# Input weights through a ring of eight slots, a second accumulator buffer, and other durations in the scheduler of a hybrid attention layer

## The chip, the cores and the metric

The kernel runs on one core of a Trainium2 chip. The metric is the device time of one launch in microseconds (us), the median of several runs. The engines are TensorE (PE in the profile; PEld is its weight load), VectorE (DVE), ScalarE (ACT), GpSimd (POOL) and SyncE (SP), which issues the DMAs. Each engine works through its own instructions in a fixed order; an instruction that has to wait holds up all that stand behind it on its engine.

## The reference

One decoder layer on x of 1024 rows (tokens) by 2048 columns, in float32:

```
h    = rms_norm(x, norm_w)
proj = h @ w_in                      # 2048 x 8208: q, k, v, gate of differential attention (8 heads),
                                     # q, k, v, z, b, a of gated DeltaNet (8 heads)
A: softmax(q1 k1) - lam * softmax(q2 k2), causal, with a relative bias, times v; rms_norm; * silu(gate)
B: causal convolution (width 4) and silu on q, k, v; q, k normalised; chunked delta rule with decay
   and beta (a triangular inverse per chunk, then a scan over the chunks); rms_norm; * silu(z)
out = rms_norm(x + concat(A, B) @ w_out, final_norm_w)
```

## The kernel before

**Startup.** x is loaded in eight blocks of 128 rows, normalised, transposed, and turned into seven right-hand operands (B11, T2, T3, T1, B21, T4, B22), each split into a high and a low float16 half.

**Input projection.** The product with w_in is made by a Strassen-like scheme: four quarter blocks of the weights (A11, A21, A12, A22, each 128 x 8 x 128 float32, 512 KB) and the sums S1 to S4 of them give seven products instead of eight. Such a group is a *job* (32 jobs, 224 products; two blocks of 128 columns each). A product is 24 matmuls of 512 columns (high by high, high by low, low by high, each over 8 row blocks) into one of two PSUM banks `prod`.

Task `weights` (line 700) prepares the operands. For each job it loads the four blocks into slots named `raw`, takes the sum of squares of each on ACT (`square`, in the trace ACT `jkw<-raw`), adds these up over the partitions with a 4-column matmul (`side<-ssq,ones`) and makes a power-of-two scale per column block; then ACT scales the blocks (`raw<-raw`), POOL makes S1 to S4, and `wsplit` makes the halves: `whi` on ACT, `wlo` (the remainder) on DVE or POOL. `wsplit` of product g waits until product g - 2 has been issued. The squares of the next job are taken between the splits of the present one: load A11 after the split of its product 2, load A21 and square A11 after that of 3, and so on (lines 727 to 742). There are six slots, one for each of A11, A21, S1, A12, A22, S2 of a job.

Task `collect` (line 843) drains a product from PSUM into four accumulators q, U, V, o on DVE, and hands the finished quarters to a consumer (`sink`).

**What the consumers do**, in the order of the jobs: DeltaNet keys (convolution, Gram matrices; at the end a triangular inverse of 62 dependent steps on DVE, tiles `A` and `tmp`, and a merge), values and gates and queries and keys of attention, written to DRAM; then attention; z; and queries and values of the DeltaNet, with the scan over 64 chunks (8 heads by 8). Attention goes through 128 units (head, block of 128 queries, map): scores into `bank` (four PSUM banks), the maximum on DVE (`nm`), the exponential on ACT (`prob`), the mixture on DVE, transposes on PE (`side`), a split (`ah`, `al`) and the product with v (`av`). The first query block of the DeltaNet (`head_state`, line 1416) waits until the last attention unit is done, because its tiles lie in memory that attention uses.

**Output projection.** The same scheme with w_out, in fp32r, then the last norm.

**What sets the order.** A planner (line 175) issues the instructions of 19 lanes of tasks one after the other, always the one that can start first by its own estimates: a cost per instruction (line 94), a time at which inputs are seen, and for a DMA its size by 360 GB/s and fixed times (line 296), with all DMAs one behind the other and at most eight under way. All of it runs while the program is built; what the chip gets is a fixed order for each engine.

Of the kernel before, what the change touches and what calls it, by code (L numbers as in the profile page):

```python
# [17 lines left out]
ALU = mybir.AluOpType  # L18
# [51 lines left out]
def parts_of(name, block):  # L70
    """A tile's name, or the names of its blocks where the planner follows these."""
# [7 lines left out]
class Op:  # L79
    """An instruction that is still to be issued."""  # L80
# [44 lines left out]
class Choice:  # L125
    """The same computation on either of two engines, the second preferred by so many microseconds."""
# [14 lines left out]
class Copy:  # L141
    """A DMA that is still to be issued."""
# [8 lines left out]
class Lane:  # L151
    """Tasks (generators of instructions and conditions) that are issued one after the other."""
# [21 lines left out]

class Planner:
    """Orders the instructions of several lanes by an estimate of when each can start."""

    def __init__(self, tc, lanes):
        self.tc, self.nc = tc, tc.nc
        self.free = dict(pe=0.0, act=0.0, dve=0.0, pool=0.0, queue=0.0, dma=0.0)  # L180
# [6 lines left out]
        self.now = 0.0  # L187
        self.margin = lambda: 0.8
# [3 lines left out]

# [24 lines left out]
    def seen(self, ends, eng):  # L217
        """When eng can see what others ended."""
        return max((t + HOP.get((e, eng), 0.0) for e, t in ends.items() if e != eng), default=0.0)

    def freed(self, name, eng):
        """When eng can see that the slot of a tile is free."""
        return max((t + HOP.get((e, eng), 0.0) for e, t in self.base.get(name.partition("@")[0], {}).items()), default=0.0)

    def ready(self, op):
        return max(self.free[op.eng], self.due(op))
# [23 lines left out]
    def pick(self, op):  # L250
        """The instruction and when it can start."""
# [10 lines left out]
    def do(self, op):  # L262
        op, t0 = self.pick(op)
        assert t0 < INF
        t1 = t0 + op.cost()
        self.free[op.eng] = t1
        self.recent[op.eng] = (op.out.name, *span(op.out), t1)
# [19 lines left out]
    def start(self, d):  # L287
# [8 lines left out]
        size = free_len(d.out) * d.out.shape[0] * 4  # L296
        t1 = max(t0 + q + 0.65, self.free["dma"]) + max(size / 360e3, 0.05)
        self.free["dma"] = t1
        self.ring = self.ring[1:] + [t1 + 0.9]
        self.wr[o] = {"dma": max(t1 + 0.8, self.wr.get(o, {}).get("dma", 0.0))}  # L300
        rd = self.rd.setdefault(i, {})
        rd["dma"] = max(t1 + 0.8, rd.get("dma", 0.0))
# [36 lines left out]
class Pool:  # L339
    """A tile pool whose slots the planner follows."""  # L340
# [29 lines left out]
def hybrid_trunk(ctx: ExitStack, tc: tile.TileContext, a, out):  # L370
# [275 lines left out]
    # (operands of the narrow product, the rows of its weights, the column group of the sum)  # L646
# [52 lines left out]

    def weights():  # L700
        cur = None
        for j in range(len(jobs) + 1):
            nxt = {"j": j} if j < len(jobs) else None
            cols = jobs[j][0] if nxt is not None else None

            def load(n):
                c, g = {"A11": (0, 0), "A12": (0, 1), "A21": (1, 0), "A22": (1, 1)}[n]
                t = nxt[n] = wp.tile([P, NH, P], F32, "raw", 6)
                dma(t, w_v[:, g * NH:(g + 1) * NH, cols[c]:cols[c] + P])

            def square(n, k):
                return act.activation(junk(D // 2).rearrange("p (a c) -> p a c", a=NH), nxt[n], AF.Square,
                                      accum_out=nxt["ssq"][:, k:k + 1])
# [1136 lines left out]
```

## Time and profile before

| | us |
|---|---|
| median of 3 runs | 2399.9 |
| lowest, highest | 2394.6, 2416.65 |
| span of the profiled execution | 2387.7 |
| PE, DVE, ACT, POOL busy | 1985.4, 1755.1, 1211.8, 1033.0 |

The profile is of one execution. Its span goes from the first to the last instruction; the measured times hold a few microseconds around it (the median of the runs is 12.2 above the span). Busy times of PE come from modelled ends of pipelined matmuls. The stages: startup to about 100 us, keys to 410, inverse and merge to 690, attention to 1493, scan to 1990 (all with products of the input projection between), output projection to the end.

### The profile page before, as it was taken

The numbers are of one execution on the slowest core, as the hardware profiler recorded it, in microseconds if no ns is written. First come the engines' busy times: TensorE is split into PE (matmuls) and PEld (weight loads), VectorE is DVE, ScalarE is ACT, GpSimd is POOL, SyncE is SP. The second block draws the span as 40 slices with busy tenths as digits, with TensorE's granted clock in tenths as the row PEclk, the third lists the DMA queues.
The fourth block names the chain that finished last, engine by engine and source line by source line (L and its number), as shares of the span: only waits on it lengthen the run. The fifth ranks groups of instructions, "written<-read, shape, count | busy, mean of one in ns | idle before, by whom it ended". The sixth has DMA issues, their size and how long they took to land.

```text
span 2387.7 us, 29240 instructions
## 1 busy us (share of the span) xinstructions
PE 1985.4 (83%) x10029; PEld 1201.5 (50%) x10029; DVE 1755.1 (74%) x2841; ACT 1211.8 (51%) x2506; POOL 1033.0 (43%) x696
## 2 busy tenths in 40 slices
PE   3778886788798879788888889978888998899986
PEld 2534443333355445444455445445555556677765
DVE  6868875999628657566677675666666768899998
ACT  6645553343346546555555555645555654333344
POOL 5633552433322322332233223424433436687885
PEclk7898998999899999899999999989999999999998
DMA  6253446332664554544445454234443444613303
GB/s 192 43 117 102 117 133 158 90 101 74 153 163 115 141 118 110 116 120 122 101 126 150 94 103 73 71 86 86 72 83 85 98 131 153 223 62 108 108 33 141
DMA packets 287044, 267.12 MB, mean 112 GB/s; under 512 B 51552, under 2 KB 225840, under 8 KB 285488
## 3 DMA queue, kind: packets, MB, share of 16 engines
q1 hardware_dynamic: 286896, 265.26, 43.6%
q8 instruction: 79, 1.29, 0.2%
q14 instruction: 69, 0.57, 0.1%
HBM read 189.66 MB, written 77.12 MB: 112 GB/s over the span
## 4 chain that ended last, share of the span: by engine, by line
DVE 34%; PE 25%; DMA 22%; ACT 7%; issue 5%; SPq 3%; POOL 3%; POOLq 0%; ACTq 0%; DVEq 0%
PE prod L273 17%; DMA raw<-in_w_in_dram 16%; PE bank L273 5%; DVE wlo L273 5%; SPq L303 3%; DVE tmp L273 3%; DVE acc L273 2%; DVE qT L273 2%; DVE A L273 2%; PE av L273 2%; PE side L273 2%; ACT jkw L273 2%; DVE whi L273 2%; DVE raw L273 1%; DVE c L273 1%
## 5 line engine op out<-in xcount | busy, mean ns | idle before, releaser
L273 PEld LDWEIGHTS <-whi 128*128 128x128 f16 x3680 | 366.7, 102 | 405.0 <-issue 85.8
L273 POOL TENSOR_TENSOR raw<-raw 128x1024 f32<-128x1024 f32 x127 | 324.1, 2559 | 126.3 <-ACT raw L273 71.6
L273 POOL TENSOR_TENSOR wlo<-raw,whi 128x1024 f16<-128x1024 f32 x78 | 183.3, 2350 | 396.2 <-ACT whi L273 384.2
L273 ACT ACTIVATE whi<-raw 128x1024 f16<-128x1024 f32 x224 | 235.0, 1050 | 106.9 <-PE prod L273 91.8
L273 PEld LDWEIGHTS <-wlo 128*128 128x128 f16 x1840 | 187.7, 102 | 198.1 <-issue 29.4
L273 ACT ACTIVATE jkw<-raw 128x1024 bf16<-128x1024 f32 x134 | 141.1, 1053 | 282.4 <-DMA raw<-in_w_in_dram 281.2
L273 DVE TENSOR_TENSOR wlo<-raw,whi 128x1024 f16<-128x1024 f32 x146 | 217.1, 1488 | 51.3 <-ACT whi L273 50.3
L273 PE MATMUL bank<-kst,qst 128*128 128x512 f32 (+3 forms) x384 | 123.6, 423 | 43.7 <-DMA kst<-kdl 19.1
L273 ACT ACTIVATE raw<-raw,sc 128x1024 f32<-128x1024 f32 x128 | 143.0, 1140 | 24.3 <-DVE sc L273 24.3
L273 PE MATMUL prod<-B21h,whi 128*128 128x512 f16 x256 | 107.0, 418 | 11.2 <-DVE V L273 11.2
L273 PE MATMUL prod<-T2h,whi 128*128 128x512 f16 (+1 forms) x280 | 104.0, 375 | 14.3 <-ACT whi L273 11.9
L273 DVE TENSOR_REDUCE nm<-bank 128x1 f32<-128x512 f32 (+2 forms) x192 | 106.6, 555 | 10.7 <-ACT prob L273 4.5
L273 PE MATMUL prod<-T2h,wlo 128*128 128x512 f16 (+1 forms) x280 | 104.3, 376 | 7.8 <-DVE wlo L273 7.8
L273 PE MATMUL prod<-T1h,whi 128*128 128x512 f16 x256 | 103.7, 405 | 6.0 <-DVE U L273 6.0
L273 PE MATMUL prod<-B21l,whi 128*128 128x512 f16 x256 | 107.7, 421 | 0.0
L273 PE MATMUL prod<-B21h,wlo 128*128 128x512 f16 x256 | 107.3, 419 | 0.0
L273 PEld LDWEIGHTS bank<-kst,qst 128*128 128x128 f32 x384 | 71.9, 208 | 66.4 <-ACT prob L273 21.0
L273 PE MATMUL prod<-T1h,wlo 128*128 128x512 f16 x256 | 103.9, 406 | 0.0
L273 PE MATMUL prod<-T2l,whi 128*128 128x512 f16 (+1 forms) x280 | 103.6, 374 | 0.0
L273 PE MATMUL prod<-T1l,whi 128*128 128x512 f16 x256 | 103.4, 404 | 0.0
L273 PE MATMUL prod<-B11h,whi 128*128 128x512 f16 (+1 forms) x280 | 101.4, 366 | 2.0 <-DVE V L273 2.0
L273 PE MATMUL prod<-B11h,wlo 128*128 128x512 f16 (+1 forms) x280 | 101.0, 365 | 2.2 <-POOL wlo L273 2.2
(458 smaller groups left out, 5477.1 us busy)
## 6 DMA issues: line engine op xcount, KB each, us to landing
raw<-in_w_in_dram SPq DMA_DIRECT2D x128, 512.0 KB, 8.8
qst<-qd SPq DMA_DIRECT2D x256, 64.0 KB, 3.2
xt<-in_x_dram SPq DMA_DIRECT2D x8, 1024.0 KB, 9.5
qd<-c SPq DMA_DIRECT2D x32, 256.0 KB, 3.5
B11h<-mixed SPq DMA_DIRECT2D x5, 1024.0 KB, 7.9
T2h<-in_w_out_dram SPq DMA_DIRECT2D x5, 1024.0 KB, 7.4
e<-grow SPq DMA_DIRECT2D x8, 512.0 KB, 10.4
kd<-y SPq DMA_DIRECT2D x8, 512.0 KB, 6.0
```

The source lines that it names most:

```text
L273: op.fn(*op.args, **op.kw)
L303: self.nc.sync.dma_start(out=d.out, in_=d.in_)
```

## The change

Three things, and the order that follows from them:

- The weight blocks go through eight slots in one sequence A11, A21, S1, A12, A22, S2 over all jobs. Eight places are taken at the start (six of them loads); each split of the products 2 to 6 of a job, and the making of S3, takes the next place, and a place of the A blocks asks for its load. The squares stay where they were.
- U gets two buffers for all jobs; before, two jobs had a second tile U1. The scratch for software DMA descriptors is set to 1024 bytes.
- The planner gets other durations: a DMA by the length of its contiguous runs, PE at half speed after little work, and one port that certain DVE and all larger POOL instructions share.

Lines with descriptions that only went away are left out.

```diff
+LAND = 0.8
...
+def transfer(d):
+
+    size = free_len(d.out) * d.out.shape[0] * 4
+    runs = [run_dram(v) if v.space == DRAM else run_of(v) for v in (d.out, d.in_)]
+    run = min(min(runs), 16384)
+    packets = size / run
+    each = 0.004 + run / 25.5e3
+    if d.in_.name.startswith('in_w_in') and run <= 512:
+        each = 0.09
+    elif run <= 512:
+        each *= 1.3
+    return max(packets * each / 16, 0.05)
...
+def ported(op):
+
+    sb = [v for v in op.aps if v.space != PSUM and free_len(v) > 1]
+    if op.eng == "pool":
+        return op.name not in ("memset", "affine_select")
+    if op.eng != "dve":
+        return False
+    if op.name in ("tensor_tensor", "scalar_tensor_tensor"):
+        return len(sb) > 1
+    return op.name in ("tensor_copy", "tensor_scalar") and bool(sb) and op.out.space != PSUM
...
+class Clock:
...
+    def run(self, t0, cost):
...
     def ready(self, op):
-        return max(self.free[op.eng], self.due(op))
+        t = max(self.free[op.eng], self.due(op))
+        if t < INF and ported(op):
+            t = max(t, self.free["port"])
+        return t
...
-        t1 = t0 + op.cost()
+        t1 = self.clock.run(t0, op.cost()) if op.eng == "pe" else t0 + op.cost()
         self.free[op.eng] = t1
+        if ported(op):
+            self.free["port"] = t1
...
-        size = free_len(d.out) * d.out.shape[0] * 4
-        t1 = max(t0 + q + 0.65, self.free["dma"]) + max(size / 360e3, 0.05)
+        t1 = max(t0 + q + 0.65, self.free["dma"]) + transfer(d)
         self.free["dma"] = t1
         self.ring = self.ring[1:] + [t1 + 0.9]
-        self.wr[o] = {"dma": max(t1 + 0.8, self.wr.get(o, {}).get("dma", 0.0))}
+        self.wr[o] = {"dma": max(t1 + LAND, self.wr.get(o, {}).get("dma", 0.0))}
         rd = self.rd.setdefault(i, {})
-        rd["dma"] = max(t1 + 0.8, rd.get("dma", 0.0))
+        rd["dma"] = max(t1 + LAND, rd.get("dma", 0.0))
...
+    RAWS = 8
+
     def weights():
+        made = {}
+
+        def state_of(j):
+            return made.setdefault(j, {"j": j}) if j < len(jobs) else None
+
+        def room(j, n):
+
+            st = state_of(j)
+            if st is None:
+                return
+            t = st[n] = wp.tile([P, NH, P], F32, "raw", RAWS)
+            if n[0] == "A":
+                c, g = int(n[2]) - 1, int(n[1]) - 1
+                c, g = {"A11": (0, 0), "A12": (0, 1), "A21": (1, 0), "A22": (1, 1)}[n]
+                c0 = jobs[j][0][c]
+                dma(t, w_v[:, g * NH:(g + 1) * NH, c0:c0 + P])
+
+        RING = ("A11", "A21", "S1", "A12", "A22", "S2")
+        place = [0]
+
+        def advance(n=1):
+            for _ in range(n):
+                j, k = divmod(place[0], len(RING))
+                place[0] += 1
+                room(j, RING[k])
+
+        def square(st, n, k):
+            return act.activation(junk(D // 2).rearrange("p (a c) -> p a c", a=NH), st[n], AF.Square,
+                                  accum_out=st["ssq"][:, k:k + 1])
+
+        def wsplit(st, idx):
+            g = 7 * st["j"] + idx
+            yield lambda: issued[0] >= g - 2
+            n = ORDER[idx][0]
+            hi = wp.tile([P, NH, P], F16, "whi", 3)
+            lo = wp.tile([P, NH, P], F16, "wlo", 3)
+            yield act.activation(hi, st[n], AF.Copy)
+            yield Choice(*(e.tensor_tensor(out=lo, in0=st[n], in1=hi, op=ALU.subtract) for e in (dve, pool)),
+                         lean=0.7)
+            ready_w[g] = hi, lo
+
+        yield when("loads")
+        advance(RAWS)
         cur = None
         for j in range(len(jobs) + 1):
-            nxt = {"j": j} if j < len(jobs) else None
-            cols = jobs[j][0] if nxt is not None else None
-
-            def load(n):
-                c, g = {"A11": (0, 0), "A12": (0, 1), "A21": (1, 0), "A22": (1, 1)}[n]
-                t = nxt[n] = wp.tile([P, NH, P], F32, "raw", 6)
-                dma(t, w_v[:, g * NH:(g + 1) * NH, cols[c]:cols[c] + P])
-
-            def square(n, k):
-                return act.activation(junk(D // 2).rearrange("p (a c) -> p a c", a=NH), nxt[n], AF.Square,
-                                      accum_out=nxt["ssq"][:, k:k + 1])
+            nxt = state_of(j)
 
             def scaled(n, c):
                 return act.activation(nxt[n], nxt[n], AF.Copy, scale=nxt["s"][:, c:c + 1])
-
-            def wsplit(st, idx):
-                g = 7 * st["j"] + idx
-                yield lambda: issued[0] >= g - 2
-                n = ORDER[idx][0]
-                hi = wp.tile([P, NH, P], F16, "whi", 3)
-                lo = wp.tile([P, NH, P], F16, "wlo", 3)
-                yield act.activation(hi, st[n], AF.Copy)
-                yield Choice(*(e.tensor_tensor(out=lo, in0=st[n], in1=hi, op=ALU.subtract) for e in (dve, pool)),
-                             lean=0.7)
-                ready_w[g] = hi, lo
 
             def either(**kw):
                 ops = [e.tensor_tensor(**kw) for e in (dve, pool)]
                 return Choice(*ops, lean=W_LEAN) if nxt["j"] == 0 else ops[1]
 
-            if j == 0:
-                yield when("loads")
             for i in range(7):
                 if cur is not None and i < 5:
                     yield from wsplit(cur, i + 2)
+                    advance()
                 if nxt is None:
                     continue
                 if i == 0:
                     nxt["ssq"] = wp.tile([P, 4], F32, "ssq", 2)
-                    load("A11")
+                    yield square(nxt, "A11", 0)
                 elif i == 1:
-                    load("A21")
-                    yield square("A11", 0)
+                    yield square(nxt, "A21", 2)
                 elif i == 2:
-                    nxt["S1"] = wp.tile([P, NH, P], F32, "raw", 6)
-                    load("A12")
-                    yield square("A21", 2)
+                    yield square(nxt, "A12", 1)
                 elif i == 3:
-                    load("A22")
-                    yield square("A12", 1)
-                elif i == 4:
-                    yield square("A22", 3)
+                    yield square(nxt, "A22", 3)
                 elif i == 5:
...
-                    s2 = nxt["S2"] = wp.tile([P, NH, P], F32, "raw", 6)
-                    yield either(out=s2, in0=nxt["S1"], in1=nxt["A11"], op=ALU.subtract)
+                    yield either(out=nxt["S2"], in0=nxt["S1"], in1=nxt["A11"], op=ALU.subtract)
                     nxt["S3"] = nxt["A21"]
                     yield either(out=nxt["S3"], in0=nxt["A11"], in1=nxt["A21"], op=ALU.subtract)
+                    advance()
                     yield scaled("A12", 0)
...
+    EV = {"q": 1, "U": 2, "V": 1, "o": 1}
+
     def ev_tile(name):
-        flags = users.get(name, [])
-        yield lambda: all(flags)
-        users[name] = []
-        return box["kp" if name == "U1" else "ev"].tile([P, 512 + HALO], F32, name)
+        history, bufs = users.setdefault(name, []), EV[name]
+        yield lambda: len(history) < bufs or all(history[-bufs])
+        history.append([])
+        return box["ev"].tile([P, 512 + HALO], F32, name, bufs)
 
     def consume(name, task):
-        flags = users[name]
+        flags = users[name][-1]
...
-        over = "U1" if j in (1, 3) else "U"
...
-            U = acc_["U"] = yield from ev_tile(over)
+            U = acc_["U"] = yield from ev_tile("U")
...
-                    acc_load(wp, "raw", 6, 0, tb, (0,))
+                    acc_load(wp, "raw", RAWS, 0, tb, (0,))
...
-    nc = bacc.Bacc("TRN2", target_bir_lowering=False, num_devices=1)
+    nc = bacc.Bacc("TRN2", target_bir_lowering=False, num_devices=1, dynamic_dma_scratch_size=1024)
```

All engines' rows move. Two places show what the prediction speaks of.

The first is SP, startup. `raw<-in_w_in_dram` are the weight loads, `xt` the blocks of x. Before:

```order
L303 DMA xt<-in_x_dram 128x2048 x2
L303 DMA gdn_w<-in_gdn_norm_w_dram 128x1
L303 DMA sub_w<-in_da_subln_w_dram 128x1
L303 DMA raw<-in_w_in_dram 128x8x128 x2
L303 DMA xt<-in_x_dram 128x2048
L303 DMA raw<-in_w_in_dram 128x8x128 x2
L303 DMA xt<-in_x_dram 128x2048 x3
L303 DMA raw<-in_w_in_dram 128x8x128 x2
L303 DMA cw<-in_conv_w_dram 96x128
L303 DMA alb<-in_a_log_dram 128x8
```

and now:

```order
L396 DMA xt<-in_x_dram 128x2048 x2
L396 DMA gdn_w<-in_gdn_norm_w_dram 128x1
L396 DMA sub_w<-in_da_subln_w_dram 128x1
L396 DMA raw<-in_w_in_dram 128x8x128 x6
L396 DMA xt<-in_x_dram 128x2048 x4
L396 DMA raw<-in_w_in_dram 128x8x128
L396 DMA cw<-in_conv_w_dram 96x128
L396 DMA alb<-in_a_log_dram 128x8
L396 DMA dtb<-in_dt_bias_dram 128x8
L396 DMA raw<-in_w_in_dram 128x8x128 x2
```

Six weight loads stand ahead of the fifth block of x, two before; with them the first two blocks of the second job are on their way, which before were asked for only in the course of the first.

The second is PE, in attention's sixth head, fifth query block (`bank<-kst,qst` are scores of 512 and 128 columns, `prod` products of the input projection, `side`, `av` and `oT` the later steps of attention). Before:

```order
L273 MATMUL av<-ident,oT 128x128 x2
L273 MATMUL side<-ident,prob 128x128
L273 MATMUL bank<-kst,qst 128x512 x2
L273 LDWEIGHTS wlo
L273 MATMUL prod<-T2h,wlo 128x512
L273 LDWEIGHTS whi
L273 MATMUL prod<-T3h,whi 128x512
L273 LDWEIGHTS whi
L273 MATMUL prod<-T3l,whi 128x512
L273 MATMUL side<-ident,prob 128x128 x3
L273 MATMUL bank<-kst,qst 128x128 x2
L273 LDWEIGHTS wlo
```

and now:

```order
L367 LDWEIGHTS wlo
L367 MATMUL prod<-T2h,wlo 128x512
L367 MATMUL bank<-kst,qst 128x512 x2
L367 MATMUL bank<-kst,qst 128x128 x2
L367 MATMUL av<-ident,oT 128x128 x2
L367 MATMUL bank<-kst,qst 128x512 x2
L367 MATMUL av<-ah,vv 128x256
L367 MATMUL bank<-kst,qst 128x128 x2
L367 MATMUL bank<-kst,qst 128x512 x2
L367 MATMUL av<-ah,vv 128x256
L367 MATMUL av<-al,vv 128x256
```

Before, the products run on between the steps of attention. Now the `prod` row here is the last for 240 rows: the remaining 128 of the 384 score matmuls, and all of attention that belongs to them, stand without a product between.

## Rows read from the trace of the kernel before

**Rows 1.** Stretch, length; busy PE, PEld, DVE, ACT, POOL (instructions); clock, DMA, GB/s.

```profile
0.00:100.00 100.00, 46.32 (x555) 41.60 (x556) 80.62 (x123) 62.32 (x108) 67.45 (x63) 0.78 0.45 129
100.00:410.00 310.00, 257.21 (x1223) 129.27 (x1219) 220.16 (x377) 156.00 (x309) 128.57 (x80) 0.91 0.50 123
410.00:690.00 280.00, 224.85 (x1151) 107.33 (x1151) 227.83 (x235) 112.58 (x151) 111.97 (x47) 0.91 0.41 107
690.00:1493.00 803.00, 685.26 (x3427) 391.26 (x3425) 526.39 (x1060) 450.00 (x1013) 230.81 (x193) 0.94 0.50 117
1493.00:1990.00 497.00, 430.03 (x2296) 268.59 (x2294) 331.82 (x606) 275.81 (x678) 203.55 (x141) 0.95 0.42 96
1990.00:2388.00 398.00, 341.76 (x1390) 263.48 (x1390) 368.32 (x442) 155.12 (x251) 290.64 (x176) 0.95 0.31 112
```

**Rows 2.** ACT's waits (total us, times, longest): span, 690 to 1493, 1493 to 1990.

```profile
ACT jkw L273 <- DMA raw<-in_w_in_dram: 281.2, 75, 12.1
ACT jkw L273 <- DMA raw<-in_w_in_dram: 117.9, 29, 8.4
ACT jkw L273 <- DMA raw<-in_w_in_dram: 44.6, 11, 12.1
```

**Rows 3.** Timeline, 830 to 849: start us, us, instruction [idle before, releaser].

```profile
830.87 0.39 SPq L303 DMA_DIRECT2D raw<-in_w_in_dram  x1
...
838.92 0.38 PE L273 MATMUL prod<-B21h,wlo 128*128 128x512 f16 x1
...
845.94 1.06 ACT L273 ACTIVATE jkw<-raw 128x1024 bf16<-128x1024 f32 x1 [7.27 <-DMA raw<-in_w_in_dram]
...
847.14 0.59 PE L273 MATMUL side<-ssq,ones 128*128 128x4 f32 x2 [6.76 <-ACT jkw L273]
...
848.59 0.65 PE L273 MATMUL prod<-B21h,wlo 128*128 128x512 f16 x1
```

**Rows 4.** DMA issues: count, KB each, median us from issue to landing.

```profile
raw<-in_w_in_dram SPq DMA_DIRECT2D x128, 512.0 KB, 8.8
```

**Rows 5.** Stretches, tile prod alone: busy PE, PEld, DVE, ACT (instructions); clock.

```profile
100.00:410.00 310.00, 231.06 (x963) 0.00 (x0) 29.27 (x40) 3.67 (x6) 0.91 0.50 123
410.00:690.00 280.00, 202.44 (x845) 0.00 (x0) 26.39 (x36) 3.37 (x5) 0.91 0.41 107
690.00:1493.00 803.00, 531.09 (x2123) 0.00 (x0) 64.87 (x89) 8.78 (x13) 0.94 0.50 117
1493.00:1990.00 497.00, 369.43 (x1407) 0.00 (x0) 43.68 (x59) 5.34 (x8) 0.95 0.42 96
690.00:791.00 101.00, 79.70 (x340) 0.00 (x0) 10.30 (x14) 1.34 (x2) 0.98 0.55 146
```

**Rows 6.** Instructions of tile wlo: ns min/median/max, first and last start us.

```profile
L273 DVE TENSOR_TENSOR wlo<-raw,whi x146: 1203/1225/3390, 75.0 to 1960.9; 128x1024 f16<-128x1024 f32 x146
```

**Rows 7.** Stretch 410 to 690, tile A (the inverse) alone: busy DVE.

```profile
410.00:690.00 280.00, 154.47 (x129) 0.91 0.41 107
```

**Rows 8.** Attention's tiles bank, side, av: busy PE, PEld, DVE, ACT.

```profile
690.00:1493.00 803.00, 123.58 (x384) 71.92 (x384) 210.76 (x432) 121.14 (x384) 0.94 0.50 117
690.00:1493.00 803.00, 57.07 (x312) 42.78 (x312) 52.56 (x92) 43.99 (x80) 0.94 0.50 117
690.00:1493.00 803.00, 106.50 (x608) 86.15 (x608) 14.87 (x31) 56.01 (x224) 0.94 0.50 117
```

**Rows 9.** DVE's waits in the attention stretch.

```profile
DVE al L273 <- ACT ah L273: 53.3, 33, 7.1
DVE bank L273 <- DMA bias<-bvec: 36.8, 7, 9.1
DVE ss L273 <- ACT jkw L273: 29.7, 18, 5.4
...
DVE U L273 <- DMA qd<-U: 5.5, 1, 5.5
```

**Rows 10.** SP's waits (the DMA queue's own), whole span.

```profile
SPq L303 <- DVE wlo L273: 73.3, 19, 20.8
```

More of the change, by code (lines that the diff above doesn't have):

```diff
@@ L172, in advance, with run_of, run_dram, __init__ @@
         return moved
+LAND = 0.8
+def run_of(ap):
+    n = 1
+    for s, k in reversed(list(ap.ap)[1:]):
+        if k == 1:
+            continue
+        if s != n:
+            break
+        n *= k
+    return 4 * n
+def run_dram(ap):
+    n = 1
+    for s, k in reversed(list(ap.ap)):
+        if k == 1:
+            continue
+        if s != n:
+            break
+        n *= k
+    return 4 * n
+def transfer(d):
[9 more added lines that the diff above has]
+    return max(packets * each / 16, 0.05)
+PORT_1 = ("tensor_copy", "tensor_scalar", "memset")
+def ported(op):
[7 more added lines that the diff above has]
+    return op.name in ("tensor_copy", "tensor_scalar") and bool(sb) and op.out.space != PSUM
+WINDOW = 3.4133
+class Clock:
+    def __init__(self):
+        self.window, self.work, self.half = 0, 0.0, True
+    def to(self, t):
+        while t >= (self.window + 1) * WINDOW:
+            share = self.work / WINDOW
+            self.half = share < (0.8 if self.half else 0.45)
+            self.window, self.work = self.window + 1, 0.0
+    def run(self, t0, cost):
+        self.to(t0)
+        t, left = t0, cost
+        while left > 1e-9:
+            edge = (self.window + 1) * WINDOW
+            rate = 0.5 if self.half else 1.0
+            d = min(left / rate, edge - t)
+            if d <= 1e-9:
+                self.to(edge)
+                t = max(t, edge)
+                continue
+            self.work += d
+            left -= d * rate
+            t += d
+            self.to(t)
+        return t
 class Planner:
@@ L179, in __init__ @@
         self.tc, self.nc = tc, tc.nc
-        self.free = dict(pe=0.0, act=0.0, dve=0.0, pool=0.0, queue=0.0, dma=0.0)
+        self.free = dict(pe=0.0, act=0.0, dve=0.0, pool=0.0, queue=0.0, dma=0.0, port=0.0)
         self.wr, self.rd, self.base, self.after = {}, {}, {}, {}
@@ L187, in __init__ @@
         self.now = 0.0
+        self.clock = Clock()
         self.margin = lambda: 0.8
@@ L225, in ready @@
     def ready(self, op):
-        return max(self.free[op.eng], self.due(op))
+        t = max(self.free[op.eng], self.due(op))
+        if t < INF and ported(op):
+            t = max(t, self.free["port"])
+        return t
     def due(self, op):
@@ L777, in weights @@
                     yield either(out=nxt["S1"], in0=nxt["A21"], in1=nxt["A22"], op=ALU.add)
-                    s2 = nxt["S2"] = wp.tile([P, NH, P], F32, "raw", 6)
-                    yield either(out=s2, in0=nxt["S1"], in1=nxt["A11"], op=ALU.subtract)
+                    yield either(out=nxt["S2"], in0=nxt["S1"], in1=nxt["A11"], op=ALU.subtract)
                     nxt["S3"] = nxt["A21"]
                     yield either(out=nxt["S3"], in0=nxt["A11"], in1=nxt["A21"], op=ALU.subtract)
+                    advance()
                     yield scaled("A12", 0)
-                else:
+                elif i == 6:
                     yield from wsplit(nxt, 1)
@@ L906, in collect @@
             drained[0] += 1
-            consume(over, sink(0, 1, U))
+            consume("U", sink(0, 1, U))
     Gc = small("Gc", [P, H, NT])
```

## The prediction

> **What bounds the kernel now.** I read four views, from coarse to fine. First the stretches of the span [rows 1]: from 100 to 1990 us TensorE (PE) is busy for 82 to 87% of each stretch, no other engine is, except VectorE (DVE) at 81% from 410 to 690. The reader is to see there that PE is idle for 118 us of the attention stretch (803 - 685.3) and that its granted clock is 0.91 to 0.95 instead of 1. Only from 1990 on, in the output projection, is DVE the engine in front (368 of 398 us).
>
> Then the waits of ScalarE (ACT) [rows 2]: it stands 281.2 us, in 75 waits of 3.75 us, because the next instruction in its order is the square of a weight block that hasn't landed. In the attention stretch this is 117.9 us, as much as PE's whole idle time; from 1493 to 1990 it is 44.6 of PE's 67 us. [...] The loads take 8.8 us from issue to landing [rows 4].
>
> **How far ahead the loads go.** In the kernel before, a block is asked for one weight split ahead of its square, and a split goes with a product. Counted in the order in which the program issues its instructions, the four blocks' loads lie 1.0, 1.0, 0.7 and 0.8 products ahead of their squares (medians). A product costs PE 79.70 us / 340 matmuls x 24 = 5.63 us at a clock of 0.98 [rows 5], so the lead is 4 to 6 us against 8.8: late as a rule. With the ring it is 4.3, 3.8, 1.4 and 1.8 products: 24, 21, 8 and 10 us. Two blocks of four are safely early, the other two just about.
>
> **What else the order changes.** The work is the same: 32 of 224 subtractions for the low half of the weights go from GpSimd (POOL) to DVE, at 1.2 us each or up to 3.4 [rows 6], 39 to 109 us over the span; I take nothing, since DVE has 276 us free in the attention stretch alone [rows 1]; in the one where it is tight (410 to 690) the sum below leaves it 80 us. The products get ahead of all else: in the issue order the key inverse starts at product 47 (before 41), attention at 102 (before 78), and the products reach number 170 and stop, because the next results wait for tiles that only the end of attention sets free. At that point 128 of 384 score matmuls are still to come, so a third of attention runs on PE with no product between, as the second piece of the order shows. Before, attention ended at product 166 and never ran alone. This is what the change costs.
>
> **The sum**, by stretches, against the span of 2387.7 (the median of the three runs, 2399.9, is 12.2 above it; I put this on top at the end).
>
> - 0 to 100: the fifth load of x now has six weight loads ahead of it instead of two. Four loads more hold it back by nothing (it is needed late) up to 4 x 8.8 us if they went one by one; x fills the time to then, I take 4: **104**.
> - 100 to the inverse: 46 products instead of 40 (963 / 24) [rows 5]. 46 x 5.63 = 259, and PE's other work there, 257.2 - 231.1 = 26 [rows 1, 5]: 285 us. For the idle time that stays I take 5%: what is left of PE's idle time beside ACT's wait for loads is nothing in the attention stretch (118 and 117.9) and 22 of 497 us, 4.5%, in the scan [rows 1, 2]. 285 / 0.95 = **300** (before 310 for fewer products).
> - Inverse and merge: 55 products instead of 35. 55 x 5.63 = 310, other PE work 224.9 - 202.4 = 22; 332 / 0.95 = **349**. DVE: 154.5 us are the inverse itself [rows 7]; the other 73 belong to 35 products, 2.1 each, so 20 more make 227.8 + 42 = 270, below 349: PE bounds it, and DVE would only if a product cost it 3.5 us (154.5 + 55 x 3.5).
> - Attention with products: 68 products and two thirds of attention. 68 x 5.63 = 383; attention's own PE time is 685.3 - 531.1 = 154 [rows 1, 5], two thirds of it 103; 486 / 0.95 = **512**. Attention begins at 753 instead of 690, but with 102 products done, not 78.
> - Attention alone: the trace of before has no such stretch. Lower bound: DVE's work on attention, 210.8 + 52.6 + 14.9 = 278 us, a third is 93 [rows 8]. Upper bound: the pace with products, 803 / 3 = 268. Between them, the waits that are attention's own (for the split, the bias loads and the sums of squares: 53.3 + 36.8 + 29.7 = 120, a third is 40) give 133 [rows 9]. That is nearest to what the stretch will hold; for the small instructions between I go to **160**.
> - Scan: 54 products instead of 58.6, and the late loads gone: 497 - 44.6 - 4.6 x 5.63 = 426; as PE work alone it would be (54 x 5.63 + 60.6) / 0.95 = 384. The scan is a chain from chunk to chunk, so I stay at the upper one: **430**.
> - Output projection: same products, a little other sharing between DVE and POOL; bounds of 5% either way of DVE's 368 (18 us), I take nothing: **398**.
>
> Sum 104 + 300 + 349 + 512 + 160 + 430 + 398 = 2253, with 12 around it **2265 us**, 5.6% below 2399.9. The second accumulator buffer takes away a wait for U that the attention stretch has once (5.5 us) [rows 9]: nothing to 6 us, taken as nothing. The smaller DMA scratch moves no instruction: all copies of both programs stand on SP.
>
> [...] After 6.8 us without work PE ran at 0.65 us a matmul instead of 0.38 [rows 3], and in the third of attention that now stands alone PE has 51 us of work for 160 us. [...]
>
> **Rivals.**
> - *The clock stays low* where attention runs alone: 2265 + 51 = 2316. For it: the clock is 0.78 in the first 100 us, where PE is busy for less than half [rows 1]. Against: DVE has more to do there than PE even so. [...]
> - *Everything goes well*: no idle time but attention's own, alone at 133, scan at 384: 100 + 285 + 332 + 486 + 133 + 384 + 398 + 12 = 2130. Against: no stretch of before is free of idle time.
> - *Attention alone keeps its old pace*: 268 instead of 160, 2373. For it: bias and key loads are exposed there. Against: in the old pace the 118 us of late weights and all products are contained.
> - *The loads are still late*: the third and fourth block have 8 to 10 us for a load that takes 8.8. If half of the 75 waits stay, 37 x 3.75 = 139, the time is 2404: no change.
> - *Slower: the ring holds up SP.* A load that must wait for its slot stands at the head of SP's queue, and behind it are the loads of queries, keys and bias. Before, SP stood 73.3 us in 19 waits for the subtraction that frees a slot, 3.9 us each [rows 10]; if all 128 loads did, that is 494 us, and with a third on the path of attention the time is 2265 + 165 = 2430. It decides from 159 us on, or 1.2 us per load. Against: queries are asked for four units ahead, and the slot that a load takes was last read a split earlier.
> - That the loads don't go earlier is excluded by the order shown.
>
> **Chances and range.** About 1% (24 us) can be told from no change here. Forecast 0.46, clock stays low 0.15, all goes well 0.15, old pace 0.06: faster together 0.82. Still late 0.10: same. SP held up 0.08: slower. The predicted time is the forecast's, 2265. Its terms alone give 2200 to 2330 (alone 133 to 211, scan 384 to 430, idle 3 to 8%). From 2160 to 2405 the range leaves out the slow rival (0.08), half of the late one and half of the one in which all goes well, some 2 in 10.
>
> **What would show it.** In the trace of the changed kernel: ACT's wait for the weight loads under 80 us instead of 281; PE's clock at 0.96 or more from 100 us up to product 170; attention's first score at about 750 us; then a stretch of 130 to 210 us without a product matmul, with DVE the busiest engine in it; after that the scan in 430 us. The step on the loads is wrong if ACT still waits over 140 us for them; the step on the stretch alone is wrong if it is over 211 or under 133 us; the stretches before are wrong if a product costs more than 6 us of them. SP waits for subtractions well over 100 us, with PE idle for the query loads, would speak for the slow rival.

## The result, and the profile after

The changed kernel takes 2301.2 us (median; 2296.2 to 2308.2), the kernel before 2397.9 beside it: ratio 0.960, 95% interval 0.955 to 0.965. I had said 2265, a ratio of 0.944. The profiled execution took 2308.2 us with a span of 2306.5.

The stretches of after, cut at the same events as [rows 1], with the stretch without products apart; columns as there:

```profile
0.00:107.00 107.00, 55.15 (x581) 48.10 (x582) 70.18 (x112) 68.08 (x119) 60.57 (x65) 0.73 0.48 130
107.00:437.00 330.00, 275.34 (x1344) 138.45 (x1343) 230.27 (x411) 171.17 (x330) 106.17 (x67) 0.91 0.51 127
437.00:789.00 352.00, 323.58 (x1616) 152.07 (x1614) 250.62 (x289) 165.16 (x222) 139.35 (x65) 0.95 0.48 120
789.00:1290.00 501.00, 476.99 (x2471) 271.57 (x2469) 354.89 (x723) 320.85 (x694) 190.51 (x150) 0.98 0.57 132
1290.00:1465.00 175.00, 105.34 (x463) 82.17 (x464) 109.89 (x282) 78.84 (x257) 12.40 (x33) 0.70 0.28 80
1465.00:1885.00 420.00, 389.81 (x2164) 246.17 (x2163) 293.93 (x594) 258.37 (x644) 157.70 (x119) 0.97 0.47 107
1885.00:2306.00 421.00, 347.85 (x1400) 275.82 (x1398) 333.58 (x453) 156.34 (x256) 259.13 (x170) 0.89 0.30 106
```

The reader is to see three things. From 437 to 1290 PE is busy for 92 and 95% of the time (before 80 and 85%). Then come 175 us in which no engine is busy for two thirds, at a clock of 0.70. And the output projection, which nothing was to touch, is 23 us longer at a clock of 0.89 instead of 0.95.

The product matmuls alone in four of these stretches, as in [rows 5]:

```profile
107.00:437.00 330.00, 251.75 (x1094) 0.00 (x0) 34.43 (x47) 4.09 (x6) 0.91 0.51 127
437.00:789.00 352.00, 302.76 (x1316) 0.00 (x0) 39.42 (x54) 5.41 (x8) 0.95 0.48 120
789.00:1290.00 501.00, 390.39 (x1630) 0.00 (x0) 49.43 (x68) 6.06 (x9) 0.98 0.57 132
1465.00:1885.00 420.00, 334.39 (x1296) 0.00 (x0) 41.20 (x56) 5.49 (x8) 0.97 0.47 107
```

Divided by 24 these are 45.6, 54.8, 67.9 and 54.0 products, at 5.5, 5.5, 5.7 and 6.2 us.

The score matmuls alone (tile `kst`), with products beside them and without:

```profile
789.00:1290.00 501.00, 76.81 (x260) 45.52 (x259) 0.98 0.57 132
1290.00:1465.00 175.00, 49.68 (x124) 28.48 (x124) 0.70 0.28 80
```

A score matmul is busy for 0.30 us in the first and 0.40 in the second.

ACT's waits for the weight loads: the span, attention with products, the scan [rows 2]:

```profile
ACT jkw L367 <- DMA raw<-in_w_in_dram: 87.5, 25, 10.0
ACT jkw L367 <- DMA raw<-in_w_in_dram: 23.1, 9, 6.8
ACT jkw L367 <- DMA raw<-in_w_in_dram: 24.1, 4, 9.8
```

They fell from 281.2 us to 87.5. A load itself now takes 9.9 us instead of 8.8 [rows 4]; it is asked for earlier, not served faster.

At the head of PE's waits (total us, times, longest) now stand:

```profile
PE prod L367 <- DVE V L367: 49.4, 3, 16.5
PE prod L367 <- ACT T4h L367: 21.6, 7, 5.0
```

The second lies in the output projection (10.4 us before). The first is three stops of 16.5 us, all between 107 and 437. The timeline shows what DVE does in one of them (PE's last work before it ends at 262.7):

```profile
267.51 0.69 DVE L367 COPY kt<-bank 128x512 f32<-128x512 f32 x1 [2.37 <-ACT jkw L367]
...
268.18 2.19 DVE L367 SCALAR_TENSOR_TENSOR e<-e,Gc,low 128x128 f32<-128x128 f32 x8
...
270.56 1.89 DVE L367 SCALAR_TENSOR_TENSOR nd<-brk,rk 128x8 f32<-128x8 f32 x1
...
272.63 2.16 DVE L367 SCALAR_TENSOR_TENSOR n<-bank,nd,e 128x128 f32<-128x128 f32 x8 [0.19 <-DVE nd L367]
...
274.78 2.32 DVE L367 SCALAR_TENSOR_TENSOR y<-V,cwT,y 128x512 f32<-128x512 f32 x3
...
278.40 0.75 DVE L367 SCALAR_TENSOR_TENSOR V<-prod,un,U 128x512 f32<-128x512 f32 x1
...
279.20 0.59 PE L367 MATMUL prod<-B21h,whi 128*128 128x512 f16 x1 [16.46 <-DVE V L367]
```

V has one buffer. The convolution of the old V (`y<-V`) must be over before a product is added into the new one, and ahead of it on DVE stands a key head's Gram work. Until `V<-prod` has run, its PSUM bank is taken and PE stands.

### The profile page after: what moved, and what is told of

It reads as the page before. It is cut to its first block, busy times and chain, and to the rows that moved or that the text cites. A ratio compares the mean times of both kernels' runs of the same rounds, so it can differ in the third digit from the quotient of the medians.

```text
span 2306.5 us, 29242 instructions
## 1 busy us (share of the span) xinstructions
PE 1974.1 (86%) x10029; PEld 1214.3 (53%) x10029; DVE 1643.4 (71%) x2859; ACT 1218.8 (53%) x2516; POOL 925.8 (40%) x668
## 4 chain that ended last, share of the span: by engine, by line
PE 55%; DVE 15%; DMA 9%; ACT 8%; POOL 6%; issue 6%; SPq 1%; ACTq 0%; DVEq 0%; POOLq 0%
PE prod L367 39%; PE bank L367 7%; PE av L367 7%; DMA raw<-in_w_in_dram 4%; DVE wlo L367 3%; PE side L367 2%; POOL raw L367 2%; ACT jkw L367 2%; SPq L396 1%; ACT whi L367 1%; ACT raw L367 1%; DMA kst<-kdl 1%; DVE nm L367 1%; DVE A L367 1%; DMA qst<-qd 1%
## 5 line engine op out<-in xcount | busy, mean ns | idle before, releaser
L367 DVE TENSOR_TENSOR wlo<-raw,whi 128x1024 f16<-128x1024 f32 x178 | 251.6, 1416 | 129.9 <-ACT whi L367 128.1
L367 ACT ACTIVATE jkw<-raw 128x1024 bf16<-128x1024 f32 x134 | 140.8, 1051 | 88.9 <-DMA raw<-in_w_in_dram 87.5
L367 POOL TENSOR_TENSOR wlo<-raw,whi 128x1024 f16<-128x1024 f32 x46 | 102.2, 2222 | 199.4 <-ACT whi L367 191.2
L367 PE MATMUL prod<-B21h,whi 128*128 128x512 f16 x256 | 102.6, 401 | 49.4 <-DVE V L367 49.4
L367 PE MATMUL prod<-B11l,whi 128*128 128x512 f16 (+1 forms) x280 | 102.9, 368 | 0.0
L367 PE MATMUL prod<-B21h,wlo 128*128 128x512 f16 x256 | 102.5, 400 | 0.0
L367 PE MATMUL prod<-B21l,whi 128*128 128x512 f16 x256 | 102.3, 400 | 0.0
L367 PE MATMUL prod<-T3h,whi 128*128 128x512 f16 x256 | 99.0, 387 | 2.6 <-ACT q L367 2.6
L367 PE MATMUL prod<-T1h,whi 128*128 128x512 f16 x256 | 98.8, 386 | 0.8 <-DVE U L367 0.8
```

The lines of the kernel that those rows point to most:

```text
L367: op.fn(*op.args, **op.kw)
```

## The experiments

Ratios are to the kernel before, run beside it on the same chip; 1% is 24 us. A score step in the expectations is one of the 96 instructions on ACT that write `prob`, counted in the issue order.

**1. The ring alone**, that is, without the new durations: ring and two buffers for U, all durations as before.

```diff
-    return max(packets * each / 16, 0.05)
+    return max(size / 360e3, 0.05)
...
 def ported(op):
+    return False
...
-        t1 = self.clock.run(t0, op.cost()) if op.eng == "pe" else t0 + op.cost()
+        t1 = t0 + op.cost()
```

> The ring of eight slots and the second accumulator buffer as in the changed kernel, the scheduler's durations as in the kernel before (copies by bytes alone, no shared port, PE at one speed). In the issue order the loads lie 3.8, 3.8, 1.7 and 1.7 products ahead of their squares; the inverse starts at product 40, attention at 74, and no stretch of attention is left without products. Theory (the gain is the loads that no longer come late; the durations cost a stretch of attention alone): ACT's wait for the weight loads under 90 us, no stretch without products, and 2387.7 less the 118 us of PE's idle time in attention and the 45 us of the scan, 2225, with 12 around it 2237; at most 2290, so below the 2301 of the change. Rival (the order from the new durations brings the gain, the late loads were hidden): 2370 to 2400 as before, with ACT's wait gone and PE idle at other waits.

2351.2 us, ratio 0.981 (0.978 to 0.984). Neither: ACT's wait is down to 38.4 us, and a third of the gain that I had tied to it came. PE's waits of before:

```profile
PE side L273 <- ACT jkw L273: 67.6, 14, 8.8
...
PE side L273 <- DVE prob L273: 16.9, 8, 4.8
...
PE prod L273 <- DVE V L273: 13.2, 4, 6.4
...
PE bank L273 <- DVE xt L273: 9.9, 5, 4.4
...
PE bank L273 <- DVE S L273: 1.0, 2, 0.6
```

and with the ring alone:

```profile
PE prod L368 <- DVE V L368: 28.0, 7, 13.2
PE side L368 <- DVE prob L368: 27.8, 11, 7.7
PE bank L368 <- DVE xt L368: 20.6, 7, 12.2
PE bank L368 <- DVE S L368: 17.8, 9, 2.5
...
PE side L368 <- ACT jkw L368: 4.2, 2, 2.6
```

The late squares cost PE 67.6 us and now 4.2; four waits for DVE grew by 53. PE's idle time in the whole span went from 402 to 378 us. (These two executions are 30 us apart, the medians 48.) In the scan, here 1460 to 1950, ACT waits for loads only 2.5 us, and yet it takes 490 us for 58.4 products (before 497 for 58.6):

```profile
1460.00:1950.00 490.00, 368.23 (x1402) 0.00 (x0) 43.68 (x59) 5.40 (x8) 0.96 0.42 95
```

**2. The durations alone.** The kernel before, with the new durations in its planner and nothing else.

```diff
-        t1 = t0 + op.cost()
+        t1 = self.clock.run(t0, op.cost()) if op.eng == "pe" else t0 + op.cost()
...
+            t = max(t, self.free["port"])
...
-        t1 = max(t0 + q + 0.65, self.free["dma"]) + max(size / 360e3, 0.05)
+        t1 = max(t0 + q + 0.65, self.free["dma"]) + transfer(d)
```

> The kernel before, with its six slots, its load order and its single accumulator, and with the new durations in the scheduler. The loads lie 0.8, 1.2, 1.1 and 1.3 products ahead of their squares (before 1.0, 1.0, 0.7, 0.8), the inverse starts at product 43, attention at 84, and 96 score steps' last quarter stands without products. Theory (loads): the ACT wait stays, 180 to 280 us, and the stretch alone is added: 2360 to 2430. Rival (durations bring the gain): 2300 to 2330, as the whole change.

2440.3 us, 1.018 (1.015 to 1.020): 1.8% slower, ACT's wait 242.5. The theory holds in kind, the time lies 10 us above its range.

**3. Two buffers for U alone**, on the kernel before:

```diff
-        over = "U1" if j in (1, 3) else "U"
...
+    EV = {"q": 1, "U": 2, "V": 1, "o": 1}
```

> The kernel before with two buffers for the accumulator U for all jobs, and nothing else; inverse at product 40, attention at 77, as before. Theory (the trace of before has only short waits for U: 5.5 us of DVE in attention, PE's waits for U's adds 9.3 and 8.9): 2380 to 2402, within 1% of before. Rival (the second buffer is a part of the gain by itself): 2340 to 2375.

2394.6 us, 1.000 (0.997 to 1.002). Without the ring and the new durations the buffer is worth nothing (the smaller scratch is in this kernel too); what experiment 1 brought needs the ring.

**4. All but the ring.** The changed kernel with the function `weights` of the kernel before.

```diff
-        advance(RAWS)
...
+                t = nxt[n] = wp.tile([P, NH, P], F32, "raw", 6)
...
+                    load("A11")
```

> The changed kernel without its ring: six slots and the old places of the loads, but the second accumulator buffer and the new durations. Loads 0.8, 1.4, 1.3 and 1.4 products ahead, inverse at product 43, attention at 84, 24 score steps without products. It is the kernel with new durations alone (2440) plus the second buffer. Theory A (ring and second buffer are each worth what taking them out of the change costs; one buffer cost 60 us): 2440 - 60 = 2380, and the ring is worth some 80 us on top of the new durations, where on the old ones ring and buffer brought 48 together. Theory B (the 60 us of the single buffer were only another order): 2420 to 2440, ring worth 120 to 140. Rival (ring worth nothing with these durations): 2300 to 2320. ACT's wait for the weight loads 200 to 260 us in all three.

2415.9 us, 1.008 (1.005 to 1.011), ACT's wait 240.0: nearer to theory B. The ring is worth 1.9% on the old durations (1.000 to 0.981) and 4.8% on the new (1.008 to 0.960). The parts don't add up: -1.9 (experiment 1) and +0.8 (this one) would make -1.1, and together they make -4.0. The second buffer is a part of this kernel and not of that of experiment 2: on the new durations without the ring it is worth 1.0% (1.018 to 1.008).

**5. One buffer for U** in the changed kernel.

```diff
-    EV = {"q": 1, "U": 2, "V": 1, "o": 1}
+    EV = {"q": 1, "U": 1, "V": 1, "o": 1}
```

> The changed kernel with one buffer for the accumulator U instead of two (before, two of the jobs had a second one under another name, so this is a little less than before). The order shifts with it: inverse at product 41 instead of 47, attention at 91 instead of 101, 32 score steps without products instead of 34. Theory (the second buffer is worth 0 to 6 us): 2295 to 2310. Rival (it is what lets the products run ahead, and a good part of the gain): 2330 or more, with PE waits for U's adds of over 25 us.

2361.0 us, 0.984 (0.980 to 0.987): the rival. PE's wait for U's adds was 24.0 us, just under its 25 and all of it in the keys' stretch, and 55.9 in 9 waits for `qT` (after 10.7, 3). I come back to it in 11.

**6. Without the port** in the planner's reckoning: it no longer makes DVE and POOL wait for each other in its estimates. The chip is the same.

```diff
 def ported(op):
+    return False
```

> The changed kernel, only that the scheduler does not reckon with one port shared by DVE and POOL; ring, copy durations and PE's two speeds stay. Inverse at product 40, attention at 80, no stretch of attention without products; 68 of 224 subtractions on POOL, not 46. Theory (it is the port's duration that delays attention until a third of it stands alone, at a clock of 0.71): the stretch alone (144 us, in which PE is busy for 90) goes, its work lies beside products, and the time falls to 2301 less 50 to 80, some 2235. Rival (attention alone costs nothing, since its chain of small steps is as long beside products): 2290 to 2310. Second rival (POOL and DVE do hold each other up, and the port kept them apart): above 2320, with mean times of the subtractions on POOL above 2.3 us and on DVE above 1.5.

2301.8 us, 0.960 (0.957 to 0.962): the same as the change, as the first rival had it, and yet another program. The stretch alone was gone and attention over at about 1420, some 40 us earlier; but the scan took 480 us for 53 products, against 420 for 54. Its stretch:

```profile
1420.00:1900.00 480.00, 405.45 (x2173) 255.08 (x2173) 334.08 (x595) 261.81 (x658) 169.89 (x123) 0.94 0.41 95
```

DVE is busy for 40 us more than in the change on the same work. Its instructions there (line, operation, shapes, count, busy us, mean ns):

```profile
L368 DVE SCALAR_TENSOR_TENSOR qT<-q,cwT,qT 128x512 f32<-128x512 f32 x24 | 45.0, 1874 | 0.8 <-ACT qT L368 0.5
...
L368 DVE TENSOR_SCALAR vr<-vr,sc 128x128 f32<-128x128 f32 x48 | 21.6, 502 | 0.1
```

and in the change (1457 to 1885):

```profile
L367 DVE SCALAR_TENSOR_TENSOR qT<-q,cwT,qT 128x512 f32<-128x512 f32 x24 | 29.4, 1223 | 0.8 <-ACT qT L367 0.5
...
L367 DVE TENSOR_SCALAR vr<-vr,sc 128x128 f32<-128x128 f32 x48 | 12.0, 285 | 0.1
```

These two make 25 of the 40 us. The timeline of this kernel shows why, first DVE's part, then POOL's:

```profile
1539.37 0.74 DVE L368 SCALAR_TENSOR_TENSOR qT<-q,cwT,qT 128x512 f32<-128x512 f32 x1
...
1540.70 2.47 DVE L368 SCALAR_TENSOR_TENSOR qT<-q,cwT,qT 128x512 f32<-128x512 f32 x1
...
1584.70 7.92 DVE L368 SCALAR_TENSOR_TENSOR qT<-q,cwT,qT 128x512 f32<-128x512 f32 x3
```

```profile
1540.49 2.12 POOL L368 TENSOR_TENSOR wlo<-raw,whi 128x1024 f16<-128x1024 f32 x1 [5.80 <-ACT whi L368]
...
1583.74 8.32 POOL L368 TENSOR_TENSOR raw<-raw 128x1024 f32<-128x1024 f32 x3 [0.48 <-ACT raw L368]
```

The same instruction took 0.74 us alone and 2.5 to 2.6 beside a POOL operation that started before it: in both places DVE ended 0.56 us after POOL (1543.17 and 1542.61; 1592.62 and 1592.06). So DVE was held up beside POOL in these places of the scan, as the second rival had it, although the time stayed under its 2320; that a shared port is the cause, and that POOL is held up too, no row here shows.

**7. The port in the scan only.** If 6 is right, port and no port each win one stretch.

```diff
+PORT_ON = [lambda: False]
 def ported(op):
+    if not PORT_ON[0]():
+        return False
...
+    PORT_ON[0] = lambda: sum(d[0] == "attend" for d in done) == 32 and drained[0] < 7 * len(jobs)
```

> The changed kernel with the shared port reckoned with only from the end of attention to the last input product. Up to there it is the kernel without the port (attention over at 1420, at 178.5 products, none of it alone), and from the last input product on too (output 403 us, the change 421). Theory (the port helped the scan, in which the change takes 7.9 us a product against 9.2 without it, and cost a stretch of attention alone and 18 us in the output): 52.5 products x 7.93 = 416 us of scan, 1420 + 416 + 403 = 2239, with what lies around the span 2235 to 2250; faster than both. Rival (the scan of the kernel without port is long because it starts with less of its own work done, or because such orders differ by chance): 2290 to 2310.

2246.6 us, 0.938 (0.935 to 0.941): the theory, and the fastest of all. Attention, scan and output:

```profile
680.00:1430.00 750.00, 678.99 (x3525) 392.67 (x3523) 538.06 (x1079) 460.05 (x1027) 229.13 (x195) 0.96 0.53 125
1430.00:1850.00 420.00, 389.22 (x2163) 245.77 (x2163) 294.40 (x597) 258.17 (x647) 155.81 (x118) 0.97 0.47 108
1850.00:2249.00 399.00, 342.92 (x1404) 264.54 (x1404) 377.27 (x449) 157.69 (x260) 288.39 (x176) 0.95 0.31 112
```

The scan takes 420 us as in the change, with DVE at 294; attention 750 with no stretch alone, some 30 us sooner over; the output 399, so that the port also made the change's 421. Reckoning with the port in the planner is worth 2.1% in the scan (0.960 to 0.938) and costs 2.2% elsewhere; in the change the two cancel. How much it costs elsewhere moves with the order, as the next run shows (by that run it is 3.9%).

**8. A nudge.** The changed kernel with one constant hardly moved, to see what chance does to an order.

```diff
-LAND = 0.8
+LAND = 0.85
```

> The changed kernel with one constant of the scheduler moved by next to nothing: 0.85 us instead of 0.8 for what a copy takes to be seen after its transfer. The inverse still starts at product 47 and attention at 100.5; 47 score steps stand without products instead of 34. It tells how much of a difference between two orders is chance. Theory (the orders differ by chance by little): 2290 to 2312. Rival (the list of instructions tips over, and such changes make 20 to 60 us): outside of it, and then the 60 us of the single accumulator buffer and the 0 us of the port are no measure of buffer and port. If the stretch alone is what costs, 13 more score steps without products at 4.2 us each (144 us / 34) are 55 us, of which the products saved elsewhere give back about half: 2325.

2339.1 us, 0.977 (0.974 to 0.981), 1.7% slower than the change. The stretch without products, which is 1265 to 1500 here:

```profile
1265.00:1500.00 235.00, 143.17 (x630) 112.03 (x630) 150.40 (x390) 106.89 (x353) 17.56 (x47) 0.70 0.29 85
```

In the traces 177 score matmuls fall into it and 124 into that of the change: 235 us / 177 = 1.33 and 175 / 124 = 1.41 us each, at the same clock of 0.70. The products come back 35 us later than in the change, and the kernel takes 38 more. So the chance seems to lie in how much of attention is left alone, with that stretch as the price; 9 tests it. By what was said before the run, the 2.4% of 5 and the nothing of 6 are then no measure of buffer and port. So 9 to 11 go by the order of 7, in which attention never stands alone.

**9. The same nudge in the kernel of 7.**

```diff
-LAND = 0.8
+LAND = 0.85
```

> The kernel with the port reckoned with in the scan alone (2247), and the same small move of one constant (0.85 us instead of 0.8) that cost the changed kernel 38 us through 13 more score steps without products. Here the order has no such steps in either version; inverse at product 40, attention at 81. Theory (the 38 us were the stretch alone, not chance of any order): 2237 to 2262. Rival (every order of this kind differs by 40 us, and 2247 was luck): 2270 or more.

2263.8 us, 0.944 (0.942 to 0.946): 0.6% above its twin, 2 us above the theory's range and below the rival's. Without a stretch alone such an order still differs by some 13 us; smaller differences below are no evidence. It is a single nudge in each kernel, so 13 us is a first measure of chance and no bound.

**10. The kernel of 7 without the ring** (the edit of 4), and, in a second kernel, with copies **by their bytes** as before:

```diff
-    return max(packets * each / 16, 0.05)
+    return max(size / 360e3, 0.05)
```

> The same kernel (port in the scan alone, second buffer, new copy durations) with six slots and the old places of the loads: 1.0, 1.6, 1.5 and 1.5 products ahead instead of 3.9, 3.8, 1.5 and 1.8; no score steps without products. ACT waits for the weight loads 200 to 260 us again. Theory (the ring is worth what it was worth under the new durations, 115 us, because the durations shorten the other waits that took the place of the late loads): 2335 to 2370. Rival 1 (it is worth the 43 us that it brought under the old durations): 2280 to 2300. Rival 2 (order by chance): below 2270.

> The kernel with the port in the scan alone, but a copy reckoned by its bytes alone as in the kernel before; ring, second buffer, PE's two speeds stay. Inverse at product 39.5, attention at 73, as in the ring alone (2351). Theory (the copy durations are what makes the stretches up to the end of attention shorter, and the port is worth some 22 us more in the scan: 59 products x 7.93 = 468 instead of 490): 2315 to 2340. Rival (the copy durations bring nothing, PE's two speeds or the ring do): 2240 to 2270.

Without the ring 2347.2 us, 0.978 (0.976 to 0.980), ACT's wait 209.7: the theory, the ring is worth 4.0% here. In the scan ACT waits 56.0 us for loads without it and 20.8 with it, and the scan takes 460 us for 53.6 products and 420 for 54.0. With the old copy durations 2302.3, 0.959 (0.957 to 0.961): these are worth 2.0%. Against the ring alone that kernel has the port in the scan and PE's two speeds, together worth 2.2% (0.981 to 0.959), not the 0.9 that I had worked out for the port; neither theory nor rival has the time, the theory is right in kind and 13 us out in size. The loads' own lead is the same with both copy durations (1.5 to 3.9 products), and ACT waits less for them with the old ones (35.2 us, 64.1 with the new), so the new ones act through the rest of the order: in 400 to 680 us PE is busy for 219 us with the old and 237 with the new.

**11. The kernel of 7 with one buffer for U** (the edit of 5).

> The kernel with the port in the scan alone and one buffer for the accumulator U. Inverse at product 37, attention at 75; no score steps without products. Theory (the 60 us that the single buffer cost the change were its waits in the scan: PE stood 55.9 us for DVE's qT and 24.0 for U, 10.7 and 0.8 in the change): 2290 to 2310. Rival (they came from the order around the stretch alone, and the buffer by itself is worth nothing, as in the kernel before): 2240 to 2262.

2291.2 us, 0.954 (0.952 to 0.957): 1.6% slower. PE's longest wait in the scan, with one buffer:

```profile
PE side L372 <- DVE qT L372: 54.4, 9, 10.1
```

and the same wait with two:

```profile
PE side L372 <- DVE qT L372: 10.4, 3, 5.3
```

The 44 us between them stand beside the 39 us (1.6%) that the kernel loses. Up to 1430 us the two run level; with one U the scan takes 450 us instead of 420 and the output 414 instead of 399. (The 24.0 us of waits for U's adds, which the expectation counts in, lay ahead of the scan in 5.)

PE's waits for `qT` in the other runs say when the buffer counts. Where the planner reckons with the port in the scan, they are 54.5 and 55.9 us with one U (2 and 5), and at most 10.7 with two (4, 8, 9, 10 and the change). Where it doesn't, a second U changes nothing: 24.2 us in the kernel before, 24.7 in 3. By the code, with one U its whole convolution (`qT<-U`) has to be issued before the next job's first add into U, and PE, whose next instructions are the transposes of `qT`, stands until it is done; with two, products can go ahead of them.

## Why the prediction was right, and where it was not

By the terms of the sum, forecast and measured: startup 104 and 107; keys 300 and 330; inverse and merge 349 and 352; attention with products 512 and 501; alone 160 and 175; scan 430 and 420; output 398 and 421. Sum 2253 and 2306. The 12 us on top weren't there: an execution takes 1.7 us more than its own span (2308.2 and 2306.5), so the 12.2 of before lay between two executions, not around the span. The median lies 7 below that execution.

- **The order** was read rightly: products 45.6, 54.8, 67.9 and 54.0 against 46, 55, 68 and 54, the first score at 789 us instead of "about 750", no product over 6 us ahead of the scan.
- **Late loads**: ACT's wait is 87.5 us, just above the 80 that I named and far below 140. But in attention I put all of PE's idle time down to it (118 and 117.9 us). Experiment 1 gives a third of the forecast gain: the next wait, for DVE, was nearly as late. The new durations, of which I had priced only what their order costs, brought the time from 0.981 to 0.960, and without the ring they cost 0.8 to 1.8% (4 and 2). That these two errors cancelled in the sum is luck.
- **Scan, -10**: right by luck too. The term takes the 44.6 us of ACT's wait off the 497 of before. Experiment 1 takes that wait away, which should have given about 450 on nearly as many products, and its scan takes 490. The 420 needs two things that the term hadn't: the port in the planner (480 without it, 6) and the second buffer (450 with one U, 11). With both in place the step on the loads holds: without the ring the scan takes 40 us more, and ACT waits 35 us more in it (10).
- **Keys, +30**: "for the idle time that stays I take 5%". PE was idle for 55 of 330 us, 17%, and 49.4 of it are the stops on V. I checked DVE's load in the inverse, not the place of V's adds in DVE's order here. No run gave V a second buffer, so that cause is read from the trace alone. The stops move with the order: between 100 and 440 us they are 31.3 us without the port (6) and 0.8 with one U (5), where PE waits 24.0 for U's adds instead and gets no more products done (46.7, in the change 47.6). PE's clock, 0.91 and 0.95 up to 789 us, fell short of my 0.96 there.
- **Attention alone, +15**: inside 130 to 210 us, with DVE the busiest engine (110 us). PE was busy for 105 us where I had put 51. The clock is the smaller part of that. My 51 is a third of a difference of busy times (685.3 - 531.1), which leaves out what overlaps a product; attention's tiles by themselves were busy for 287 us [rows 8], 96 to the third. At the pace of 789 to 1290, at a clock of 0.98, the tiles `kst`, `side` and `av` of this stretch would have been busy for 95 us (an estimate from their counts); they were for 124, at 0.70. In slices of 10 us the granted clock lay between 0.50 and 0.88, up and down from slice to slice. That a low clock doubles PE's 51 us, from which the rival's 2316 and the 211 of the range come, was my assumption, and no run shows it: the tiles' busy time was 1.3 times the estimate (124 and 95 us). The stretch took 15 us more than my 160, not 51. That the rival's 2316 is nearer to the result than my 2265 is chance: keys and output, which it had as I had them, were 53 us longer.
- **Output, +23**: "same products, a little other sharing" was wrong. The port orders this stage too: PE waits 21.6 us for T4h and 13.8 for T1h (before 10.4 and 2.4), at a clock of 0.89. Without it, the stage takes 399 (7) and 403 (6).
- **The second buffer**: "nothing to 6 us". Nothing alone (experiment 3); in the change 2.4% (5) and in the kernel of 7 1.6%, 39 us (11). It is the step that failed most plainly: its price was read from a kernel in which the wait that it takes away isn't there. In these runs PE's long waits for `qT` come only with one U and the port in the planner together (11).
- **The slow rival** did not bite: SP waited 134.1 us for subtractions instead of 73.3 [rows 10], but PE only 7.6 us for queries in attention.

What stays open: which waits the copy durations remove (of PE's, no single one changes by as much as 20 us), what PE's two speeds in the planner do by themselves, which was not tried, and how far orders differ by chance, for which there is one nudge in each of two kernels.

## What to carry to other kernels

Removing the longest wait pays the difference to the next one: list what PE waits for behind it before giving the whole of it to the sum. Where a planner sets the order, change one of its durations at a time and in one stage at a time: a truer duration can win one stage and lose as much in another, and a nudge without meaning shows how far to trust a difference. The stretch in which PE had only a chain of small steps cost twice here, in waits (PE busy for 105 of 175 us) and in the clock (0.70 after 0.98). And a difference of two busy times isn't the work of what is left: take the tiles' own.

## What the runs showed of the hardware

- A DVE `scalar_tensor_tensor` of 128 x 512 with three tensors in SBUF (two read, one written; a column of scalars beside them) took 0.74 us, and 2.5 to 2.6 beside a POOL operation that began before it (`qT<-q,cwT,qT` in the scan of experiment 6).
- In the stretch without products, where PE works in pieces with stops between, its granted clock was 0.70 (175 us) and 0.70 again (235 us, experiment 8), between 0.50 and 0.88 in slices of 10 us of the first; in the 501 us ahead of the first it was 0.98.
- A 512 KB weight load took 9.9 us from issue to landing in the change and 8.8 before. Without the ring, under the new durations, it took 8.9 to 9.5 (2, 4, 10), so the ring isn't all of it.
